# The channel stage of the Fourier branch placed ahead of the recurrence, with its sine block 256 columns wide

## The chip, the cores and the metric

The kernel runs on one core of a Trainium2 chip. The metric is the device time of one execution in microseconds (us); lower is better. The engines are TensorE (PE in the rows, with its weight loads as PEld), VectorE (DVE), ScalarE (ACT), GpSimd (POOL) and SyncE (SP), which here issues the data transfers (DMAs). Each works through its own list of instructions in a fixed order and waits where an operand or a buffer is not ready.

## What is computed

One encoder layer, applied with the same weights to two sequences: the prompt (512 positions) and the sample (1024 positions), 1024 features each. Cut to the part that matters here:

```python
h = rms_norm(x, g_pre_mix) * (1 + sc1) + sh1          # modulation from silu(c) @ w_ada
xa, ya, xb, ga, gb = split(h @ w_in)
xa    = depthwise_conv(xa, conv_w, conv_b, left=2)     # width 4
h_fwd = rg_lru(xa, ..., reverse=False)                 # a first-order recurrence over positions,
h_bwd = rg_lru(xa, ..., reverse=True)                  # gates from two 128x128 products per head
y_a   = ((h_fwd + h_bwd) * gelu(ya)) @ w_a_out
y_b   = fourier_mix(xb) @ w_b_out                      # real 2-D DFT over (positions, 128 channels of a group)
x     = x + gt1 * rms_norm((sigmoid(ga)*y_a + sigmoid(gb)*y_b) @ w_o, g_post_mix)
# then a second sub-layer: h @ w_up, width-3 conv, gelu(gate)*value, @ w_down, norm, gate, residual
```

## The kernel before

All products are made with fp32 data in three passes. An operand is split into a rounded high part and the rest (`split`): the high part is written by ScalarE (L109) or VectorE (L111, a cast), the low part always by VectorE (L112, a subtraction). A pass is high x high, high x low or low x high.

The program is a list of steps. A step is one weight tile ("unit", 128 x 1024 fp32, 512 KB), its matmuls (`mm`) and what is done with the result (`post`). `emit` writes the steps out one after the other into all engines' lists at once. When it comes to a step it first prepares (splits) the units up to three steps ahead, and raw tiles are loaded some further ahead. So the place of a step in the list fixes the order of its work on every engine, and an instruction that waits holds up all that follow it on its engine. Tiles in memory come from a pool of 40 shared buffers (`big`), tiles of TensorE results from a pool of four (`ps`). All DMAs of weights and activations go through SP's list.

The mixer of each sequence is built by `mix` as one list of steps, in this order:

- `mix_heads`: per group of features (4 groups for the prompt, 8 for the sample) a projection to the recurrence input (`w_xa`, then the convolution, L649 on ScalarE and L657 on VectorE), one for each of the gates of the merge (`w_ga`, `w_gb`; L736 on ScalarE, then written out to memory), and a recurrence step (`lru_step`). That has its matmuls, tanh, exp and square root on ScalarE and, put off by up to one step, products and two scans on VectorE (L702, L705, L714 to L722).
- `pq_steps`, the channel stage of the Fourier branch: four steps. For each feature block the positions of the projected rows are paired, x[t] + x[n-t] and x[t] - x[n-t] (`pair_up`: VectorE L800, L803, L804, the high part by ScalarE L109, the low part by VectorE L112). The paired blocks `eh`, `el` are the stationary operand against a table `wxb` (made at the start from the input weights, `wxf`, and written to memory). Each of 8 feature blocks takes, per 128 output positions, three matmuls on the cosine columns (260) and three on the sine columns (252), and three matmuls of one row of output. The rows `hr` are loaded by `ld` (L832). Its results, `pq`, wait for `dft_steps`.
- `ya_steps`: the gelu gate of the recurrence output (`w_ya`), ready for the merge.
- `dft_steps`: the transform over positions, from `pq`.

After that come `merge_steps` (the outputs of both branches, L986 to L997) and the output projection. Within `pq_steps`, the pairing of step j is attached to the step that stands two before it (`PAIR_AHEAD`), and its load to the step three before it.

For the sample, 34 steps of another kind (`ada_steps`, which multiply the conditioning for the later gates on VectorE, L337) are put between the mixer's steps by a list of positions (`place`).

Of the kernel before, what the change touches and what calls it, by code (L numbers as in the profile page):

```python
# [11 lines left out]
F32R = mybir.dt.float32r  # L12
AF = mybir.ActivationFunctionType
# [7 lines left out]
DFF = 2816  # L21
FT = DFF // 128
GRP = 4
NPQ = 512
NCOS = 260
HALF = 258
WIDE = 1032
# [45 lines left out]
class Enc:  # L73
# [175 lines left out]
    def setup(self):  # L249
        nc, a = self.nc, self.a  # L250
        self.hrow = {q.name: self.dram([KT, 128, q.n], "hrow" + q.name) for q in (self.p, self.s)}
        self.wxb = self.dram([KT, 128, NPQ], "wxb")
        self.ident = self.const.tile([128, 128], F32, name="ident")
# [135 lines left out]
    def fold_in(self, tiles, out, ks):  # L389
        nc = self.nc  # L390
        for k in ks:
            ps = self.ps([128, 2, 512])
            v = ps[:, 0, :].rearrange("p (g c) -> p g c", g=4)
            for g in range(4):
                self.mmul(
                    v[:, g, :], lhsT=tiles[g][:, k * 128:(k + 1) * 128], rhs=self.fold,
                    start=True, stop=True)
            w = self.big([128, NPQ], name="wxf")
            nc.scalar.activation(
                out=w[:, 0:252].rearrange("p (g c) -> p g c", g=4), in_=v[:, :, 0:63], func=AF.Copy)  # L400
            nc.scalar.activation(
                out=w[:, 260:512].rearrange("p (g c) -> p g c", g=4), in_=v[:, :, 65:128], func=AF.Copy)
            nc.vector.tensor_copy(w[:, 252:260].rearrange("p (a g) -> p g a", a=2), v[:, :, 63:65])
            out.append(w)

# [334 lines left out]
    def mix_heads(self, sq, hb, hs, sig, lead=0):  # L740
        xh, xl = (lambda: hb["hi"]), (lambda: hb["lo"])
        xc = {}

        def tiles(g):
            return range(g * sq.nf, (g + 1) * sq.nf)

        def proj(nm, g, post):
            return self.fm_steps(sq, self.a[nm], tiles(g), xh, xl, post, on_act=sq.nf == 1)

        fill = [(nm, g, self.spill_post(sig[w, g])) for g in range(sq.groups) for w, nm in enumerate(("w_ga", "w_gb"))]  # L750
        jobs = []
        for g in range(sq.groups):
            jobs.append(("w_xa", g, lambda ps, g=g: self.conv_a(sq, ps, g, xc)))
            jobs.append(fill.pop(0))
            if g:
                jobs += [g - 1, fill.pop(0)]
        jobs += fill[:1] + [sq.groups - 1] + fill[1:]
        steps = []
        for j in jobs[lead:]:
            if isinstance(j, int):  # L760
                steps.append(self.lru_step(sq, j, xc, hs))
            else:
                steps += proj(*j)
        return jobs[:lead], steps
# [53 lines left out]
    def pq_steps(self, sq, pq, before):  # L818
        nc = self.nc
        steps = []  # L820
        n, nt = sq.n, sq.pq_tiles
        box, eo = {}, []
        parts = (slice(0, NCOS), slice(NCOS, NPQ))
        rows = {}

        def ld(j):
            def f():
                rows[j] = []
                for i in range(2 // sq.nf):
                    k = 2 * j + i  # L830
                    x = self.big([128, sq.nf, n + 2], name="hr")
                    nc.sync.dma_start(  # L832
                        out=x[:, :, 0:n], in_=self.hrow[sq.name][k:k + sq.nf].rearrange("k p n -> p k n"))
                    rows[j].append(x)
            return f

        def pair(j):
            return lambda: self.pair_up(sq, rows.pop(j), eo)
        for j in range(KT // 2):
            u = Unit(self.wxb[2 * j:2 * j + 2].rearrange("k p c -> p k c"), 2 * NPQ, on_act=True)  # L840

            def mm(u=u, j=j):
                if j == 0:
                    box["ps"] = [self.ps([128, 2, 512]) for _ in range(nt // 2 + 1)]
                    box["out"] = [box["ps"][t // 2][:, t % 2, :] for t in range(nt)]
                    box["row"] = box["ps"][-1][0:1, 0, 0:NCOS]
                for i in range(2):
                    k = 2 * j + i
                    hi, lo = eo.pop(0)
                    wh, wl = u.hi[:, i * NPQ:(i + 1) * NPQ], u.lo[:, i * NPQ:(i + 1) * NPQ]  # L850
                    end = k == KT - 1
                    for t in range(nt):
                        for c, cols in enumerate(parts):
                            x = slice(t * 128, (t + 1) * 128)
                            for q, (l, r) in enumerate(((hi, wh), (hi, wl), (lo, wh))):
                                self.mmul(
                                    box["out"][t][:, cols], lhsT=l[:, c, x], rhs=r[:, cols],
                                    start=(k == 0 and c == 0 and q == 0), stop=(end and c == 1 and q == 2),
                                    skip_group_check=True)
                    for q, (l, r) in enumerate(((hi, wh), (hi, wl), (lo, wh))):  # L860
                        self.mmul(box["row"], lhsT=l[:, 1, 0:1], rhs=r[:, 0:NCOS],
                                  start=(k == 0 and q == 0), stop=(end and q == 2))

            def post():
                for t in range(nt):
                    pq[t] = self.big([128, 2, NPQ], F32R, name="pq")
                self.split_all([(pq[t], box["out"][t]) for t in range(nt)])
                r = self.big([1, NCOS], name="row")
                nc.scalar.activation(out=r, in_=box["row"], func=AF.Copy, scale=0.5 / math.sqrt(n))
                pq["row"] = self.big([1, 2, NCOS], F32R, name="rowhl")  # L870
                self.split(pq["row"][:, 0, :], pq["row"][:, 1, :], r)
                box.clear()
            steps.append(Step(mm=mm, unit=u, post=post if j == KT // 2 - 1 else None))
        for j in range(KT // 2):
            st = (before + steps)[len(before) - PAIR_AHEAD + j]
            st.post = self.both(st.post, pair(j))
            st = (before + steps)[len(before) - PAIR_AHEAD - 1 + j]
            st.post = self.both(st.post, ld(j))
        return steps
# [508 lines left out]
def place(main, side, at):  # L1388
    out = []
    side = list(side)  # L1390
    at = sorted(at)
    for i, s in enumerate(main):
        while at and at[0] <= i and side:
            at.pop(0)
            out.append(side.pop(0))
        out.append(s)
    return out + side
# [3 lines left out]
def encoder(ctx: ExitStack, tc: tile.TileContext, a, outs):  # L1401
    nc = tc.nc
    e = Enc(ctx, tc, a, outs)
    p, s = e.p, e.s
# [3 lines left out]
    with tc.manual_schedule():  # L1408
# [5 lines left out]
        pq = {q: {} for q in "ps"}  # L1414
# [3 lines left out]
        fo = {q: {} for q in "ps"}  # L1418

        def mix(q, heads):  # L1420
            out = heads
            out += e.pq_steps(q, pq[q.name], heads)
            out += e.ya_steps(q, h1[q.name], hs[q.name], yb[q.name])
            out += e.dft_steps(q, pq[q.name], z[q.name])
            return out

        first, heads = e.mix_heads(p, h1["p"], hs["p"], sig["p"], lead=3)
        side = [e.cond_step()] + e.ada_steps(2) + [Step(), Step()] + e.gate_steps(p, 0, gate["p", 0])
        steps = mix(p, heads)
        ya = len(steps) - 10  # L1430
        sa, sbt = e.h_steps(s, a["x_sample"], 0, h1["s"])
        steps += weave(e.merge_steps(p, yb["p"], z["p"], sig["p"], mg["p"]), sa, 1, 1)
        steps = place(steps, side, [ya - 10] + [ya + i // 2 for i in range(16)] + [ya + 10] + [ya + 22] * 9)
        steps += weave(e.rows_steps(p, a["w_o"], mg["p"], gate["p", 0], a["x_prompt"], x2["p"]), sbt, 0, 1)

        _, heads = e.mix_heads(s, h1["s"], hs["s"], sig["s"])
        steps += place(mix(s, heads), e.ada_steps(3) + e.ada_steps(4), [*range(28), *range(36, 46)])
        pa, pbt = e.h_steps(p, x2["p"], 1, h2["p"])
        steps += weave(e.merge_steps(s, yb["s"], z["s"], sig["s"], mg["s"]),
                       e.gate_steps(s, 0, gate["s", 0]) + pa, 8, 1)  # L1440
# [126 lines left out]
```

## Time and profile before

| | us |
|---|---|
| median of 3 runs | 2152.92 (2151.53 to 2154.18) |
| the profiled execution, its own time | 2154.59 |
| its span, first to last instruction | 2152.8 |
| TensorE busy | 2086.5 (97%) |
| VectorE busy | 1433.5 (67%) |
| ScalarE busy | 928.4 (43%) |
| GpSimd busy | 54.5 (3%) |

The profiled execution is one run, so durations taken from it are to be set against its own 2154.59 us, of which 1.8 us lie outside the span. "Busy" counts an engine as busy while an instruction of its own is under way; matmuls overlap and their ends are modelled, so the distance between the starts of successive matmuls is the better measure of their cost. A mark such as `[8.51 <-ACT th L683]` behind a row says that the engine stood idle 8.51 us before it and what released it. PEclk is the clock granted to TensorE as a share of full speed.

### The profile page before, as it was taken

Reading aid. Unit: us, or ns where it says so; the run is one execution under the profiler, and the core shown is the slowest. Engines: PE = TensorE matmul, PEld = TensorE weight load, DVE = VectorE, ACT = ScalarE, POOL = GpSimd, SP = SyncE. Lnnn points to the kernel's source line nnn. Section 1 sums busy time; section 2 is a strip of 40 time slices with the busy share of each in tenths; the row PEclk is TensorE's granted clock in tenths of the full one; section 3 lists DMA queues with packets and bytes.
Section 4 is the critical chain, followed back from the end, with each engine's and each line's share of the span. In section 5 each row is a group of like instructions: output and inputs, shape, how many; then the busy total and the mean of one; then the engine's idle time right before and its main releaser. Section 6 shows DMA issues by size and latency. Waiting matters only on the chain.

```text
span 2152.8 us, 24316 instructions
## 1 busy us (share of the span) xinstructions
PE 2086.5 (97%) x9602; PEld 1704.4 (79%) x9602; DVE 1433.5 (67%) x1816; ACT 928.4 (43%) x1195; POOL 54.5 (3%) x124
## 2 busy tenths in 40 slices
PE   7997799999999789999999999999999999999998
PEld 6886688888888668888888888888888888888887
DVE  4785788666776654656757546557788888875543
ACT  2447345345646532224533334643334444454442
POOL 0000010100000000000000000100000000000000
PEclk9998799999999889999999999999999999999999
DMA  9444366533232321453544323432122222285422
GB/s 340 155 147 146 113 227 217 202 108 112 85 99 92 130 86 59 148 175 111 184 155 137 108 98 125 140 127 88 50 88 79 79 81 86 72 300 176 162 93 107
DMA packets 91121, 284.52 MB, mean 132 GB/s; under 512 B 9056, under 2 KB 20736, under 8 KB 91008
## 3 DMA queue, kind: packets, MB, share of 16 engines
q1 hardware_dynamic: 91008, 282.98, 38.2%
q8 instruction: 75, 1.23, 0.2%
q14 instruction: 38, 0.31, 0.0%
HBM read 237.84 MB, written 45.11 MB: 131 GB/s over the span
## 4 chain that ended last, share of the span: by engine, by line
PE 90%; DVE 4%; ACT 3%; issue 1%; DMA 1%; POOL 0%; SPq 0%; DVEq 0%; POOLq 0%; ACTq 0%
PE ps L201 89%; PE ps L204 1%; ACT th L683 1%; DVE hl L112 0%; DVE th L714 0%; DVE th L719 0%; ACT th L693 0%; DVE el L112 0%; ACT eh L109 0%; ACT ea L691 0%; DMA hr<-hrowp 0%; DVE th L717 0%; DMA wxbt<-in_wxbT_dram 0%; DVE eo L804 0%; ACT xn L412 0%
## 5 line engine op out<-in xcount | busy, mean ns | idle before, releaser
L201 PE MATMUL ps<-hh,hl 128*128 128x512 f32 x2144 | 631.8, 394 | 0.0
L201 PEld LDWEIGHTS ps<-hh,hl 128*128 128x128 f32 x2144 | 402.4, 188 | 94.7 <-DVE hl L112 0.2
L201 PE MATMUL ps<-hl,ah 128*128 128x512 f32 x1440 | 453.1, 396 | 0.0
L112 DVE TENSOR_TENSOR hl<-raw,hl 128x1024 fp32r<-128x1024 f32 (+2 forms) x240 | 287.3, 1200 | 163.9 <-ACT hl L109 161.4
L201 PE MATMUL ps<-hl,hl 128*128 128x512 f32 x1072 | 380.7, 394 | 0.0
L201 PE MATMUL ps<-hx,wq 128*128 128x512 f32 x1596 | 370.7, 394 | 0.0
L201 PEld LDWEIGHTS ps<-hx,wq 128*128 128x128 f32 x1596 | 299.6, 188 | 71.0 <-DVE wq L1248 0.2
L109 ACT ACTIVATE hl<-raw 128x1024 fp32r<-128x1024 f32 x204 | 213.6, 1053 | 265.6 <-PE ps L201 238.5
L201 PEld LDWEIGHTS ps<-hl,ah 128*128 128x128 f32 x1440 | 268.9, 188 | 62.2
L201 PE MATMUL ps<-hl,al 128*128 128x512 f32 x720 | 283.9, 394 | 0.0
L201 PEld LDWEIGHTS ps<-hl,hl 128*128 128x128 f32 x1072 | 201.3, 188 | 47.2
L201 PEld LDWEIGHTS ps<-hl,al 128*128 128x128 f32 x720 | 135.2, 188 | 32.3
L1344 DVE SCALAR_TENSOR_TENSOR cf<-ps,vec,cf 128x511 f32<-128x511 f32 (+1 forms) x100 | 75.3, 808 | 83.6 <-ACT cf L1336 83.3
L201 PE MATMUL ps<-yh,hl 128*128 128x512 f32 x384 | 112.3, 395 | 0.6 <-DVE hl L112 0.5
L201 PE MATMUL ps<-hl,eh 128*128 128x260 f32 (+2 forms) x224 | 58.7, 363 | 43.3 <-ACT eh L109 30.4
L1192 DVE SCALAR_TENSOR_TENSOR cf<-cq,vec,cf 128x1023 f32<-128x1023 f32 x76 | 97.1, 1277 | 0.0
L1247 ACT ACTIVATE wq<-wsum 128x512 fp32r<-128x512 f32 x76 | 46.1, 629 | 118.0 <-DVE wsum L1258 118.0
L201 PEld LDWEIGHTS ps<-yh,hl 128*128 128x128 f32 x384 | 71.5, 188 | 17.8 <-DVE hl L112 1.0
L1336 ACT ACTIVATE cf<-ps,vec 128x512 f32<-128x512 f32 (+1 forms) x50 | 39.1, 826 | 105.6 <-PE ps L201 105.6
L201 PEld LDWEIGHTS ps<-hl,eh 128*128 128x128 f32 (+1 forms) x224 | 46.5, 250 | 47.7 <-ACT eh L109 32.5
L112 DVE TENSOR_TENSOR al<-fq,ah 128x512 fp32r<-128x512 f32 x88 | 57.2, 686 | 35.2 <-PE ps L201 18.5
L736 ACT ACTIVATE sg<-ps 128x1024 f32<-128x1024 f32 x24 | 24.7, 1028 | 114.1 <-PE ps L201 114.0
(181 smaller groups left out, 2432.8 us busy)
## 6 DMA issues: line engine op xcount, KB each, us to landing
raw<-in_w_up_dram SPq DMA_DIRECT2D x88, 512.0 KB, 3.5
raw<-in_w_down_dram SPq DMA_DIRECT2D x66, 512.0 KB, 3.5
ada<-in_w_adaT_dram SPq DMA_DIRECT2D x32, 512.0 KB, 4.7
raw<-in_w_o_dram SPq DMA_DIRECT2D x24, 512.0 KB, 3.5
fs<-cf SPq DMA_DIRECT2D x22, 512.0 KB, 2.6
fq<-fs SPq DMA_DIRECT2D x22, 512.0 KB, 6.4
ada<-in_w_ada_dram SPq DMA_DIRECT2D x16, 512.0 KB, 8.7
raw<-in_w_gb_dram SPq DMA_DIRECT2D x16, 512.0 KB, 4.3
```

The lines of the kernel that those rows point to most:

```text
L109: nc.scalar.activation(out=hi, in_=src, func=AF.Copy)
L112: nc.vector.tensor_tensor(out=lo, in0=src[:, 0:keep], in1=hi[:, 0:keep].bitcast(F32), op=ALU.subtract)
L201: self.nc.tensor.matmul(*args, **kw)
L204: self.nc.tensor.transpose(*args)
L683: nc.scalar.activation(out=t[:, f, :], in_=ps[:, f, :], func=AF.Tanh, scale=0.5, bias=self.halfb[:, b:b + 1])
L736: self.nc.scalar.activation(out=t, in_=ps, func=AF.Tanh, scale=0.5)
L1192: nc.vector.scalar_tensor_tensor(out=box[key][:, o], in0=c[:, i], scalar=self.vec[:, V_FW + 3 * m + t:V_FW + 3 * m + t + 1], in1=box[key][ ...
L1247: nc.scalar.activation(out=hi, in_=src, func=AF.Copy)
L1336: nc.scalar.activation(out=acc[:, f, :], in_=ps[:, f, :], func=AF.Identity, scale=w[:, 1:2], bias=self.vec[:, V_FB + m:V_FB + m + 1])
L1344: nc.vector.scalar_tensor_tensor(out=acc[:, f, o], in0=ps[:, f, o.start + d:o.stop + d], scalar=w[:, tap:tap + 1], in1=acc[:, f, o], op0=A ...
```

## The change

Four things. The channel stage is no longer put behind all heads but behind the first four head steps of the prompt and the first three of the sample, so that its pairing and loads are attached to those. The sine columns of the table are moved from 260:512 to 264:516, with four zero columns (written by GpSimd) ahead of them; the sine matmul reads 256 columns and writes result columns 256:512, where the zeros are added to the last four cosine columns. In the prompt's job list two entries are exchanged (the first recurrence step and the projection that followed it), so that the first four prompt steps hold no recurrence. And the positions of the conditioning steps in the sample's list are shifted.

```diff
-NPQ = 512
+NPQ = 516
...
-                out=w[:, 260:512].rearrange("p (g c) -> p g c", g=4), in_=v[:, :, 65:128], func=AF.Copy)
+                out=w[:, 264:516].rearrange("p (g c) -> p g c", g=4), in_=v[:, :, 65:128], func=AF.Copy)
+            nc.gpsimd.memset(w[:, 260:264], 0.0)
...
         jobs += fill[:1] + [sq.groups - 1] + fill[1:]
+        if lead:
+            jobs[4], jobs[5] = jobs[5], jobs[4]
...
-        parts = (slice(0, NCOS), slice(NCOS, NPQ))
+        parts = ((slice(0, NCOS), slice(0, NCOS)), (slice(NCOS, NPQ), slice(256, 512)))
...
-                        for c, cols in enumerate(parts):
+                        for c, (wcols, cols) in enumerate(parts):
...
-                                    box["out"][t][:, cols], lhsT=l[:, c, x], rhs=r[:, cols],
+                                    box["out"][t][:, cols], lhsT=l[:, c, x], rhs=r[:, wcols],
...
-            out = heads
-            out += e.pq_steps(q, pq[q.name], heads)
+            at = 4 if q is p else 3
+            out = heads[:at] + e.pq_steps(q, pq[q.name], heads[:at]) + heads[at:]
...
-        steps += place(mix(s, heads), e.ada_steps(3) + e.ada_steps(4), [*range(28), *range(36, 46)])
+        steps += place(mix(s, heads), e.ada_steps(3) + e.ada_steps(4), [0, 1, 2, *range(7, 34), *range(36, 46)])
```

The counts of instructions are the same on TensorE, VectorE, ScalarE and SP; GpSimd has eight more. What moves, on TensorE, in the prompt: before, the channel stage (operands `eh`, `el`) follows the matmuls of the last recurrence step (`xch`, `xcl`).

```order
L201 MATMUL ps_1674<-xcl_1361,hl_1532 128x512
L201 MATMUL ps_1674<-xch_1360,hl_1532 128x512
L201 MATMUL ps_1716<-hl_1563,eh_1631 128x260 x2
L201 MATMUL ps_1716<-hl_1563,el_1632 128x260
L201 MATMUL ps_1716<-hl_1563,eh_1631 128x252 x2
```

Now it follows the projection for the second merge gate (`hh`, `hl` are the parts of the normalised input).

```order
L201 MATMUL ps_904<-hh_735,hl_835 128x512 x2
L201 MATMUL ps_904<-hl_736,hl_835 128x512
L201 MATMUL ps_904<-hh_735,hl_835 128x512
L201 MATMUL ps_986<-hl_865,eh_933 128x260 x2
L201 MATMUL ps_986<-hl_865,el_934 128x260
L201 MATMUL ps_986<-hl_865,eh_933 128x256 x2
```

The two pieces show the same stage start some 360 rows earlier in TensorE's list, behind a gate projection.

On VectorE, in the prompt: before, the pairing (L800 to L804 and the low part `el`) stands between pieces of the last recurrence step (L702 to L722).

```order
L804 TENSOR_TENSOR eo_1697<-hr_1635 128x2x256
L112 TENSOR_TENSOR el_1701<-eo_1697,eh_1700 128x1024
L702 SCALAR_TENSOR_TENSOR th_1655<-th_1655,xc_1351 128x1024
L702 SCALAR_TENSOR_TENSOR th_1675<-th_1675,xc_1351 128x1024
L705 SCALAR_TENSOR_TENSOR th_1655<-ea_1684,th_1655 128x1024
L705 SCALAR_TENSOR_TENSOR th_1675<-ea_1690,th_1675 128x1024
L112 TENSOR_TENSOR hl_1711<-raw_1566,hl_1711 128x1024
L800 COPY hr_1704<-hr_1704 128x2
L803 TENSOR_TENSOR eo_1749<-hr_1704 128x2x256
L804 TENSOR_TENSOR eo_1749<-hr_1704 128x2x256
L112 TENSOR_TENSOR el_1753<-eo_1749,eh_1752 128x1024
L714 TENSOR_TENSOR th_1655<-th_1655,th_1645 128x1024
```

Now only splits of units (`hl`) stand between two pairings.

```order
L112 TENSOR_TENSOR hl_865<-raw_801,hl_865 128x1032
L112 TENSOR_TENSOR hl_899<-raw_820,hl_899 128x1032
L803 COPY hr_896<-hr_896 128x2
L806 TENSOR_TENSOR eo_930<-hr_896 128x2x256
L807 TENSOR_TENSOR eo_930<-hr_896 128x2x256
L112 TENSOR_TENSOR el_934<-eo_930,eh_933 128x1024
L112 TENSOR_TENSOR hl_940<-raw_838,hl_940 128x1032
L803 COPY hr_937<-hr_937 128x2
```

And the last recurrence step of the prompt now stands among the units of `ya_steps` and the conditioning steps (L337); lines from L400 on have moved by one to three.

```order
L112 TENSOR_TENSOR hl_1830<-raw_1738,hl_1830 128x1024
L703 SCALAR_TENSOR_TENSOR th_1846<-th_1846,xc_1558 128x1024
L703 SCALAR_TENSOR_TENSOR th_1866<-th_1866,xc_1558 128x1024
L706 SCALAR_TENSOR_TENSOR th_1846<-ea_1875,th_1846 128x1024
L706 SCALAR_TENSOR_TENSOR th_1866<-ea_1881,th_1866 128x1024
L112 TENSOR_TENSOR hl_1892<-raw_1769,hl_1892 128x1024
L337 SCALAR_TENSOR_TENSOR adap_1897,mod<-ada_1694,cs_1497 128x1024
L715 TENSOR_TENSOR th_1846<-th_1846,th_1836 128x1024
L718 SCALAR_TENSOR_TENSOR th_1836<-ea_1875,th_1846 128x512 x2
L715 TENSOR_TENSOR th_1866<-th_1866,th_1856 128x1024
L720 SCALAR_TENSOR_TENSOR th_1856<-ea_1881,th_1866 128x512 x2
```

What was beside the pairing before is thus beside the gelu gate's units now.

On SP, in the prompt, the loads of the paired rows (`hr`) now stand behind four table tiles, each of which waits for a raw buffer.

```order
L124 DMA raw_838<-wxb 128x2x516
L124 DMA raw_868<-wxb 128x2x516
L835 DMA hr_896<-hrowp 128x2x512
L738 DMA sgp_68<-sg_803 128x1024
L124 DMA raw_902<-in_w_lru_p_dram 128x1024
```

Before, the first load of `hr` also stood behind the fourth table tile; there it was issued beside the last recurrence step, now beside the gate projections.

## Rows read from the trace of the kernel before

**Rows 1.** The page's chain that ended last: shares of the span by engine

```profile
PE 90%; DVE 4%; ACT 3%; issue 1%; DMA 1%; POOL 0%; SPq 0%; DVEq 0%; POOLq 0%; ACTq 0%
```

**Rows 2.** Stretches: length, PE, PEld, DVE, ACT, POOL busy (counts), clock, DMA share, GB/s

```profile
195.36:247.82 52.46, 27.04 (x122) 23.36 (x121) 28.96 (x32) 25.11 (x31) 0.00 (x0) 0.64 0.42 143
719.24:776.13 56.89, 35.66 (x217) 32.87 (x217) 36.90 (x44) 27.45 (x28) 0.00 (x0) 0.73 0.36 118
247.82:308.06 60.24, 60.24 (x279) 49.47 (x277) 50.09 (x82) 24.33 (x31) 2.21 (x4) 1.00 0.51 173
...
776.13:900.00 123.87, 123.87 (x622) 104.17 (x621) 59.01 (x85) 32.13 (x42) 0.00 (x0) 1.00 0.28 95
```

**Rows 3.** TensorE's timeline, sample's channel stage: start, duration, engine, line, tiles, idle before

```profile
749.55 0.63 PE L201 MATMUL ps<-hl,eh 128*128 128x252 f32 x2
...
750.19 0.64 PE L201 MATMUL ps<-hl,eh 128*128 128x260 f32 x2
...
753.77 0.41 PE L201 MATMUL ps<-hl,eh 128*128 128x260 f32 x2
...
754.13 0.40 PE L201 MATMUL ps<-hl,eh 128*128 128x252 f32 x2
...
754.49 0.28 PE L201 MATMUL ps<-hl,eh 128*128 128x260 f32 x1
```

**Rows 4.** TensorE's timeline, a start in each channel stage that waited long

```profile
204.05 0.80 PE L201 MATMUL ps<-hl,eh 128*128 128x260 f32 x2 [8.51 <-ACT th L683]
...
766.05 0.80 PE L201 MATMUL ps<-hl,eh 128*128 128x260 f32 x2 [8.93 <-ACT eh L109]
```

**Rows 5.** VectorE's timeline, one pairing of the prompt

```profile
199.31 0.17 DVE L800 COPY hr<-hr 128x2 f32<-128x2 f32 x1 [6.92 <-DMA hr<-hrowp]
...
203.07 1.22 DVE L112 TENSOR_TENSOR hl<-raw,hl 128x1024 fp32r<-128x1024 f32 x1
204.21 0.16 DVE L800 COPY hr<-hr 128x2 f32<-128x2 f32 x1
```

**Rows 6.** Timelines of ScalarE and VectorE in the first prompt heads

```profile
83.67 1.03 ACT L736 ACTIVATE sg<-ps 128x1024 f32<-128x1024 f32 x1 [9.64 <-PE ps L201]
...
85.91 0.69 DVE L111 CAST hl<-raw 128x1024 fp32r<-128x1024 f32 x1
```

**Rows 7.** Timeline of ScalarE in the first sample heads

```profile
429.93 1.03 ACT L736 ACTIVATE sg<-ps 128x1024 f32<-128x1024 f32 x1 [9.93 <-PE ps L201]
...
441.07 1.21 ACT L649 ACTIVATE xc<-ps,vec 128x1024 f32<-128x1024 f32 x1 [9.17 <-PE ps L201]
```

**Rows 8.** SP's timeline, first load of hr; summary line of all 12 loads

```profile
191.69 0.46 SPq L832 DMA_DIRECT2D hr<-hrowp  x1
...
DMA to landing us min/median/max: 3.2/4.7/9.9
```

**Rows 9.** VectorE's timeline, one recurrence step of the prompt

```profile
89.63 2.36 DVE L702 SCALAR_TENSOR_TENSOR th<-th,xc 128x1024 f32<-128x1024 f32 x2
...
97.03 1.22 DVE L705 SCALAR_TENSOR_TENSOR th<-ea,th 128x1024 f32<-128x1024 f32 x1 [2.98 <-ACT ea L691]
...
101.35 1.23 DVE L714 TENSOR_TENSOR th<-th,th 128x1024 f32<-128x1024 f32 x1 [1.23 <-ACT th L709]
...
109.62 0.69 DVE L111 CAST hl<-raw 128x1024 fp32r<-128x1024 f32 x1
```

**Rows 10.** VectorE's timeline, the merge's first product of the prompt

```profile
308.26 1.22 DVE L997 SCALAR_TENSOR_TENSOR mg<-sg,ps 128x1024 f32<-128x1024 f32 x1
```

**Rows 11.** VectorE's timeline, the convolution in the first sample heads

```profile
442.31 3.92 DVE L657 SCALAR_TENSOR_TENSOR xc<-ps,vec,xc 128x1022 f32<-128x1022 f32 x3 [8.01 <-ACT xc L649]
...
448.14 1.22 DVE L112 TENSOR_TENSOR hl<-raw,hl 128x1024 fp32r<-128x1024 f32 x1
```

**Rows 12.** Groups of GpSimd by form: one of its four memsets

```profile
L1556 POOL MEMSET const-bfloat16-1.0<- 128x1 bf16 x1 | 0.1, 102 | 0.0
```

**Rows 13.** Waits of SP's queue: total, times, longest

```profile
SPq L832 <- PE ps L201: 8.1, 1, 8.1
```

More of the change, by code (lines that the diff above doesn't have):

```diff
@@ L865, in post @@
                 for t in range(nt):
-                    pq[t] = self.big([128, 2, NPQ], F32R, name="pq")
+                    pq[t] = self.big([128, 2, 512], F32R, name="pq")
                 self.split_all([(pq[t], box["out"][t]) for t in range(nt)])
```

## The prediction

> **What bounds the kernel now.** I read the chain that ended last first: TensorE holds 90% of it [rows 1], so the time is what TensorE needs plus what it waits. The list of TensorE's waits by length leads to two places with waits above 8 us, 204.05 in the prompt and 766.05 in the sample [rows 4], both in the channel stage. The reader is to see that one waits for ScalarE's tanh of a recurrence step (its result buffers are taken) and the other for a high part of a pairing. The stretches of the two channel stages then give their size [rows 2]: in the prompt 52.46 us with TensorE busy for 27.04 at a mean clock of 0.64, in the sample 56.89 us with 35.66 at 0.73. Right behind each, TensorE is busy without a gap at clock 1.00.
>
> How much of this is needed? At full clock six matmuls start within 754.49-753.77 = 0.72 us, three on 260 columns (0.36 to 754.13) and three on 252 (0.36): 0.12 us each [rows 3]. While the clock is at its lower level (1.2 of 2.4 GHz), after waits, three take 750.19-749.55 = 0.64, or 0.215 each. The prompt has 8 blocks x (2 tiles x 2 halves x 3 + 3) = 120 matmuls, 14.4 us; the sample 8 x (4 x 2 x 3 + 3) = 216, 25.9 us. So 38.1 and 31.0 us are lost, 69.1 together: the most that any placing of this stage can give.
>
> The loss has a plain cause. One pairing runs 3.76 us from its copy to the end of its low part (199.31 to 203.07, with ScalarE's high part in the middle), and with one unit's low part behind it the next begins at 204.21, 4.9 us later [rows 5]. The prompt needs four, the sample eight. 4 x 4.9 is 20 us and not 52: the rest is recurrence work in between on VectorE's and ScalarE's lists.
>
> **The change part by part.** All from the profiled execution, 2154.59 us, 1.67 above the median of the runs.
>
> *Prompt, the stage itself.* Now it follows two gate projections. The first ends at about 83.65 (ScalarE's eviction starts at 83.67 [rows 6]); a group of 48 matmuls on 512 columns takes 441.07-429.93 = 11.1 us in the sample [rows 7] and has the same count here, so TensorE is free at 94.8. VectorE ends the split before at 85.91 [rows 6] and writes two low parts of 1.14 by 88.2. The first hr load stands on SP's queue behind the fourth table tile, which waits for the first of those low parts, so it is issued near 87.5. The like load took 199.31-191.69 = 7.6 us until VectorE could go on [rows 5, 8], so the first pairing starts at 95.1 and the second, one pairing and one low part later, at 100.0. The third load stands behind a tile whose buffer is freed at 100.0; between the median landing of 4.7 [rows 8] and 7.6 I take 6.2, so it starts at 106.2, and the fourth at 111.1. The last low part is there at 114.9, and 28 matmuls (3.4 us) follow: 118.3, which makes 23.5 us after 94.8 against 52.46: 29.0 saved. With landings of 3.2 throughout the stage takes 17.8 us, with 9.9 it takes 29.5 [rows 8]: 34.7 to 23.0 saved.
>
> *Prompt, what becomes late.* First, the recurrence steps come closer: two groups and the step's own matmuls (22.2 + 5.55 us) lie between the first and the second. In such a step VectorE stands 2.98 and 1.23 us for ScalarE [rows 9], which reaches TensorE where nothing else is left to do: 0 to 4.2, I take 2.4. Second, the last recurrence step's VectorE work, 4.7 us (four of about 1.2) and 109.62-101.35 = 8.27 [rows 9], 13.0 in all, was beside the pairings and now lies beside the gelu gate's units. There VectorE is already busy for 50.09 of 60.24 us [rows 2], so 10.15 are free: between 2.9 us (all free time is used) and 13.0 (none is) come back to TensorE as late splits, since TensorE has no gap of its own there. Units are split three steps ahead, which lets it use some of it; I take the middle, 8.0. Third, the merge's products wait at 308.26 for VectorE [rows 10]; if it is still late then, up to the 4.7 of the first half of a recurrence step, taken as 2.4. So 12.8 come back (2.9 to 21.9), and the prompt gains 16.2.
>
> *Sample.* The projection before the stage ends at 441.07 [rows 7], and VectorE idles 8.01 us before the convolution that follows it at 442.31 [rows 11]. The first step's pairings can be made in that time (the loads are issued a step earlier), so its 54 matmuls run at once, to 447.5. VectorE is in the convolution and its split until 448.14 [rows 11]; then six pairings of 3.76 and two low parts of 1.14 end at 473.0, and 25 matmuls at 476.0. That is 34.9 us against 56.89: 22.0 saved, less about 1 for matmuls at the lower clock after waits. If it all ran at that clock (216 x 0.215 = 46.4) 10.5 would be saved; if nothing waited, 31.0. What is moved behind it, the last recurrence step beside the gelu gate, has cover: VectorE is busy for only 59.01 of 123.87 us there [rows 2]. I take 21.0.
>
> *The wider sine block.* 4 more columns on 48 matmuls of the prompt and 96 of the sample. 252 and 260 columns take the same 0.36 us per three [rows 3], so I take 0; in proportion to columns it would be 144 x 0.12 x 4/256 = 0.27 us, and a gain of the like size is possible below. The table's tiles grow by 0.8%, in transfers that are not waited for. Eight small memsets of about 0.10 us [rows 12] stand on GpSimd in the lead-in, nothing waits for GpSimd there but the norms: 0, at most 0.8.
>
> The Trainium skill (SBUF — State Buffer, section "Who interferes with whom") says that GpSimd and VectorE share one pair of ports under an exclusive lock. The memsets could thus hold VectorE's copies in the lead-in for as long as they last, 0.8 us; with that the sum would be 36.4 and not 37.2. No row of before has such a memset beside a VectorE copy.
>
> *Sum.* 16.2 + 21.0 + 0 = 37.2. 2154.59 - 37.2 = 2117.4 for a profiled execution, and 1.67 less for the median: **2115.7 us**.
>
> **The rivals.**
>
> *VectorE gives little back.* If the three-step lead covers all but the 2.9 and neither other wait comes, the prompt gains 26.1 and the sample 22.0: 2104.8. For it: TensorE had no gap at all in 247.82 to 308.06 although VectorE was 83% busy. Against: the work comes in one block of 8.27 us.
>
> *VectorE gives much back.* All 21.9 of the prompt's bounds (7.1 left), and the sample midway to the lower clock (16.3): 2129.5. For it: in-order lists pass every block on. Against: all three must happen.
>
> *Everything is hidden.* The pairings vanish beside the gate projections and both stages run at their bare 14.4 and 25.9: 69.1 less, 2083.8. For it: VectorE's 8.01 idle before 442.31. Against: the stage is too short for its pairings, 20 and 30 us of VectorE. The Trainium skill (Perfetto Trace Analysis, section "Optimization Strategy") says that regimes with different busiest engines gain by interleaving; by that rule alone one would expect this case, and rows 2 show such regimes, but the stage is still in one piece.
>
> *Slower: the shared buffers run short.* The pq tiles are now held through the recurrence steps, four tiles and two rows in the sample, and every recurrence step takes eight or more buffers of the same 40. If a load waits for one in each of the 12 recurrence steps that now follow, it decides from 37.2/12 = 3.1 us per step. The one buffer wait of this kind on SP was 8.1 us [rows 13]; at that, 97.2 - 37.2 = 60.0 us slower, 2212.9. Against: the rows of hr and pairs go earlier, and those are most of what the stage holds.
>
> *The change doesn't do what it says.* The wait only moves: loads behind raw tiles make the early stage as long as the late one was. Then 2152.9. Against: even landings of 9.9 leave 29.5 us.
>
> **How the numbers follow.** Forecast 0.50 (own range 2106 to 2126); little given back 0.20; much given back 0.18; everything hidden 0.03; buffers short 0.05; no effect 0.04. The ends of the bounds are (34.7 - 2.9) + 31.0 = 62.8 and (23.0 - 21.9) + 10.5 = 11.6, that is 2090.1 and 2141.3; the range for 8 in 10 is a little inside, 2096 to 2139. Faster by over 0.2% (about 4.3 us, what a measurement of this kernel can tell from no change): the first four, 0.91; within it 0.04; slower 0.05.
>
> **What would show it.** TensorE's channel stage of the prompt near 95 to 118 us and of the sample near 441 to 476, with waits for el, eh and hr there and none for a recurrence's tanh. The pairing's starts 4.9 to 6.2 us apart in the prompt. Then waits of TensorE for low parts of units (hl) in the prompt's gelu stage of 8 us in all, where there are none now; 10 us or more in the whole prompt speaks for my give-back, under 4 for the first rival, over 18 for the second. No gap in the sample's gelu stage. The forecast is wrong if TensorE's waits behind the moved stages exceed the 50 us saved in them, or if SP shows buffer waits of over 3 us in the recurrence steps.

## The result and the profile after

The changed kernel takes 2118.6 us (median) against about 2153 before: a ratio of 0.984 with an interval of 0.9818 to 0.9863. The forecast was 2115.7. One execution of each kernel, of 2634.8 and 2308.9 us, was in a slower state and is left out. By the medians the gain is 34.3 us; the profiled executions stand 2154.59 - 2118.58 = 36.0 us apart, since the one before lies 1.67 above its median. The forecast's sum was 37.2. The kernels of the experiments are compared with 2118.6 and with runs of the kernel before beside them (2152.9 to 2153.0).

The two stretches of the channel stage, with the gelu stage of the prompt between them, in the profile after (columns as in [rows 2]):

```profile
93.41:117.44 24.03, 17.84 (x121) 15.68 (x121) 18.14 (x24) 7.15 (x8) 0.00 (x0) 0.86 0.63 210
...
225.00:289.78 64.78, 57.81 (x255) 45.95 (x254) 54.12 (x74) 30.42 (x38) 1.37 (x2) 0.97 0.43 152
...
425.98:461.32 35.34, 28.73 (x215) 26.28 (x214) 26.16 (x35) 11.50 (x13) 0.00 (x0) 0.95 0.36 130
```

The prompt's stage fell from 52.46 to 24.03 us and the sample's from 56.89 to 35.7 (425.62 to 461.32 by the starts of its first matmul and of the next step's). ScalarE is busy for only 7.15 us in the first, where it was busy for 25.11: the recurrence is gone from it. But the gelu stage, without a gap at clock 1.00 before, now has 7 us of gaps at a clock of 0.97 (it starts at 220.15, 4.9 us ahead of the stretch shown).

VectorE's pairings in the prompt, one row for the start of each (timeline; compare the 199.31 row of [rows 5]):

```profile
94.02 0.17 DVE L803 COPY hr<-hr 128x2 f32<-128x2 f32 x1 [6.86 <-DMA hr<-hrowp]
...
99.04 0.17 DVE L803 COPY hr<-hr 128x2 f32<-128x2 f32 x1
...
104.02 0.16 DVE L803 COPY hr<-hr 128x2 f32<-128x2 f32 x1
...
110.04 0.17 DVE L803 COPY hr<-hr 128x2 f32<-128x2 f32 x1 [0.31 <-DMA hr<-hrowp]
```

The reader is to see a chain with nothing else in it but one unit's split per pairing, and ahead of it 6.86 us in which VectorE waits for a load. The third load was not late; the fourth hardly.

TensorE's first wait in the prompt's stage, and some of its longer waits behind the stage (timeline):

```profile
96.71 0.80 PE L201 MATMUL ps<-hl,eh 128*128 128x260 f32 x2 [3.14 <-ACT eh L109]
...
149.62 0.47 PE L201 MATMUL ps<-xch,hl 128*128 128x512 f32 x1 [1.45 <-DVE xc L658]
...
246.02 0.80 PE L201 MATMUL ps<-hh,hl 128*128 128x512 f32 x1 [2.90 <-DVE hl L112]
...
277.65 0.73 PE L201 MATMUL ps<-yh,hl 128*128 128x512 f32 x2 [1.50 <-DVE hl L112]
...
295.85 0.39 PE L201 MATMUL ps<-z,hl 128*128 128x258 f32 x1 [0.70 <-DVE mg L1000]
...
300.82 0.50 PE L201 MATMUL ps<-yh,hl 128*128 128x512 f32 x1 [1.20 <-DVE yb L991]
```

From 149 on all of these name VectorE: the price of the move, none over 3 us. All of TensorE's waits from 117.44 up to the sample's mixer make 11.65 us; two of them, 0.28 and 0.64, name ScalarE.

What stands on VectorE ahead of the longest of them, at 246.02, is the second half of the last recurrence step and behind it a conditioning product (L337), and only then the low part that TensorE waits for:

```profile
235.33 1.23 DVE L715 TENSOR_TENSOR th<-th,th 128x1024 f32<-128x1024 f32 x1
...
243.60 1.22 DVE L337 SCALAR_TENSOR_TENSOR ada<-ada,cs 128x1024 f32<-128x1024 f32 x1
...
244.74 1.22 DVE L112 TENSOR_TENSOR hl<-raw,hl 128x1024 fp32r<-128x1024 f32 x1
```

From 235.33 to 243.60 that half takes the 8.27 us of [rows 9]. In the sample the convolution still stands on VectorE between the first step's pairings and the rest:

```profile
427.06 3.92 DVE L658 SCALAR_TENSOR_TENSOR xc<-ps,vec,xc 128x1022 f32<-128x1022 f32 x3 [1.95 <-ACT xc L650]
...
432.88 0.15 DVE L803 COPY hr<-hr 128x1 f32<-128x1 f32 x1
```

To see where the 36 us come from, the same events are looked up in both traces: ScalarE's first eviction of the prompt's recurrence input, its first of the sample's, and the sample's last gelu. Before:

```profile
66.96 1.45 ACT L649 ACTIVATE xc<-ps,vec 128x512 f32<-128x512 f32 x2 [4.07 <-PE ps L201]
...
418.79 1.21 ACT L649 ACTIVATE xc<-ps,vec 128x1024 f32<-128x1024 f32 x1 [8.42 <-PE ps L201]
...
865.33 1.03 ACT L773 ACTIVATE gl<-ps 128x1024 f32<-128x1024 f32 x1 [7.69 <-PE ps L201]
```

and after:

```profile
65.84 1.45 ACT L650 ACTIVATE xc<-ps,vec 128x512 f32<-128x512 f32 x2 [4.12 <-issue]
...
403.49 1.21 ACT L650 ACTIVATE xc<-ps,vec 128x1024 f32<-128x1024 f32 x1 [8.74 <-PE ps L201]
...
830.08 1.02 ACT L776 ACTIVATE gl<-ps 128x1024 f32<-128x1024 f32 x1 [7.74 <-PE ps L201]
```

The distance of the first two, the prompt's mixer and projection, fell from 351.8 to 337.7 (14.2), that of the last two from 446.5 to 426.6 (20.0). 1.1 us stem from the lead-in, whose work is not touched but for eight memsets and a table 4 columns wider, and 1.0 from all that stands behind the last event. That makes the 36.2 us between the two spans, 2152.8 and 2116.6.

### The profile page after: what moved, and what is told of

Same layout as the page of the kernel before. It is cut to its first block, busy times and chain, and to the rows that moved or that the text cites. A ratio compares the mean times of both kernels' runs of the same rounds, so it can differ in the third digit from the quotient of the medians.

```text
span 2116.6 us, 24327 instructions
## 1 busy us (share of the span) xinstructions
PE 2073.9 (98%) x9602; PEld 1691.0 (80%) x9602; DVE 1433.9 (68%) x1816; ACT 929.2 (44%) x1195; POOL 53.7 (3%) x132
## 3 DMA queue, kind: packets, MB, share of 16 engines
q8 instruction: 75, 1.23, 0.2%
## 4 chain that ended last, share of the span: by engine, by line
PE 78%; issue 0%; DVE 0%; ACT 0%; DVEq 0%; POOLq 0%; POOL 0%; ACTq 0%
PE ps L201 77%; PE ps L204 1%; ACT eh L109 0%; DVE el L112 0%; DVE eo L806 0%; DVE eo L807 0%; DVE ro L1099 0%; DVEq L1565 0%; POOLq L1565 0%; ACT junk L1080 0%; POOL sm L1082 0%; ACTq L1565 0%; DVE hr L803 0%; DVEq L806 0%; ACTq L109 0%
## 5 line engine op out<-in xcount | busy, mean ns | idle before, releaser
L109 ACT ACTIVATE hl<-raw 128x1024 fp32r<-128x1024 f32 (+1 forms) x204 | 213.9, 1053 | 267.8 <-PE ps L201 236.5
L201 PE MATMUL ps<-hx,hl 128*128 128x512 f32 x288 | 67.0, 394 | 0.0
L201 PE MATMUL ps<-yl,hl 128*128 128x512 f32 x192 | 65.4, 394 | 0.8 <-DVE yl L112 0.8
```

The source lines that it names most:

```text
L109: nc.scalar.activation(out=hi, in_=src, func=AF.Copy)
L201: self.nc.tensor.matmul(*args, **kw)
```

## The experiments

The theory: a channel stage lasts as long as VectorE and ScalarE need for its pairings and for what stands between them in their lists; away from the recurrence that is less, and part of it comes back where VectorE is short of time.

**The parts of the change.** The wide sine block at the old place (`NPQ`, the memset, `parts` and the pq tiles as in the change, nothing else):

> The wider sine block alone, at the old place. Theory (the gain is the channel stage taken away from the recurrence's work): no difference, 2153.5 within 2 us of the kernel before. Rival (the 256 columns or the shifted table speed the matmuls up): 144 sine matmuls would have to gain 35 us, about 0.24 us each, so a time near 2120.

2152.84 us, ratio to the kernel before 0.9998 (0.9988 to 1.0008). The width, its memsets and the larger table cost and bring nothing that can be measured, which here means no more than about 2 us.

The move with the sine block left at 252 columns:

> The move with the exchange of two entries and the shifted conditioning steps, but the sine block 252 columns wide as before. Theory: as the changed kernel, 2118.6 within 2 us. Rival (the width matters): clearly above 2120.

2118.41 us, ratio 0.9838 (0.9823 to 0.9852): the whole gain is the move.

One sequence at a time:

```diff
-            at = 4 if q is p else 3
+            at = 4 if q is p else len(heads)       # prompt alone; conditioning positions as before
```

> Changed kernel with the sample's channel stage and conditioning positions back at the old place. Theory: the prompt's part alone, by the sample's first convolution in the two traces 418.79 - 403.49 = 15.3 us less than before, so 2138. Rival (the gain is in the sample, the prompt gives all back in the gelu stage): 2150 or more.

2140.97 us, ratio 0.9943 (0.9929 to 0.9958): 12.0 us, some 3 less than expected, but far from the rival's 2150. Between the events above the prompt has its 14.0 us here too (337.87); the sample, left as it was, takes 1.0 us longer than before (447.58).

```diff
-            at = 4 if q is p else 3
+            at = len(heads) if q is p else 3       # sample alone; jobs[4], jobs[5] not exchanged
```

> Changed kernel with the prompt's channel stage and job order back as before. Theory: 35 - 15.3 = about 20 us less than before, so 2133. Rival (both parts share one gain, for example through the clock): not additive with the prompt's part, 2125 or 2145.

2130.9 us, ratio 0.9897 (0.9882 to 0.9912). The two parts bring 12.0 and 22.0 us, together 34.0, and both at once 34.3: they add up, so the rival of one shared gain fell, and the sample's is the larger.

**What makes a stage long.** The exchange of two entries undone, so that a recurrence step stands ahead of the prompt's stage:

```diff
-        if lead:
-            jobs[4], jobs[5] = jobs[5], jobs[4]
...
-            at = 4 if q is p else 3
+            at = 5 if q is p else 3
```

> Changed kernel without the exchange of two entries: in the prompt the first recurrence step stands ahead of the channel stage (gate, recurrence, gate, channel stage). Theory (VectorE's recurrence work between the pairings makes the stage long): its 13 us of VectorE work stand before the first pairing, which would start near 109 instead of 94 while TensorE is ready at 99, so the prompt's stage takes 31 to 33 us instead of 24 and the time is 2125 to 2128. Rival (any place ahead of the other recurrences is as good): 2118.6 within 2 us.

2126.88 us, ratio 0.9878 (0.9863 to 0.9892), 8.3 us above the changed kernel. The size is as expected, the picture a little different: the first pairing was to start near 109, and it starts at 101.29. VectorE's timeline in that kernel:

```profile
103.91 1.22 DVE L112 TENSOR_TENSOR el<-eo,eh 128x1024 fp32r<-128x1024 f32 x1 [1.12 <-ACT eh L109]
106.27 1.23 DVE L715 TENSOR_TENSOR th<-th,th 128x1024 f32<-128x1024 f32 x1 [1.15 <-ACT th L710]
107.53 2.34 DVE L718 TENSOR_TENSOR_SCAN th<-ea,th 128x512 f32<-128x512 f32 x2
...
113.40 1.22 DVE L723 TENSOR_TENSOR th<-th,th 128x1024 f32<-128x1024 f32 x1
...
115.68 0.16 DVE L801 COPY hr<-hr 128x2 f32<-128x2 f32 x1
```

The recurrence's second half stands behind the first pairing and not ahead of it, and TensorE waits for the second:

```profile
118.31 0.80 PE L201 MATMUL ps<-hl,eh 128*128 128x260 f32 x2 [6.91 <-ACT eh L109]
```

This is the wait of [rows 4] in small: recurrence work between two pairings. The stage lasts from 100.5 (103.92 less its wait of 3.41) to 133.99, 33.5 us, against 24.0 without it.

**What comes back, and why.** The 16 conditioning products of the prompt's gelu stage cut to 64 columns:

```diff
+                c = slice(0, 64 if job == 2 else 1024)
                 nc.vector.scalar_tensor_tensor(
-                    out=out, in0=w, scalar=0.5, in1=self.cvec[s], op0=ALU.mult, op1=ALU.mult,
+                    out=out[:, c], in0=w[:, c], scalar=0.5, in1=self.cvec[s][:, c], op0=ALU.mult, op1=ALU.mult,
```

> Changed kernel in which the 16 conditioning products that stand in the prompt's gelu stage run over 64 instead of 1024 columns (so that conditioning vector is wrong): about 16 x 1.15 = 18 us less VectorE work there, nothing else changed. Theory (what comes back in the prompt is VectorE short of time in the gelu stage and behind it): TensorE's waits there of 7.5 us and the merge's 2.7 go, the time falls to 2109. Rival (they come from ScalarE's part of the last recurrence step, or from the units' place): 2118.6 within 2 us.

2110.91 us, ratio 0.9805 (0.979 to 0.9819), 7.7 us below the changed kernel. Of TensorE's waits in the gelu and merge stages one of more than 0.6 us is left, the first:

```profile
245.30 0.50 PE L201 MATMUL ps<-hh,hl 128*128 128x512 f32 x1 [1.87 <-DVE hl L112]
```

What came back in these two stages was, but for this wait at most, VectorE's lack of time: the units' place and ScalarE's part of the last recurrence step, the rivals, are as in the changed kernel. The same without leaving anything out, by placing those products one to a step from eight steps earlier:

```diff
-... [ya - 10] + [ya + i // 2 for i in range(16)] + [ya + 10] + [ya + 22] * 9)
+... [ya - 10] + [ya - 8 + i for i in range(16)] + [ya + 10] + [ya + 22] * 9)
```

> Changed kernel in which the prompt's 16 conditioning products stand one to a step from eight steps before the gelu stage on, instead of two to a step within it: half of them, 8 x 1.22 = 10 us of VectorE work, leave the stage. Theory (VectorE has about 7.5 us too much to do in the gelu stage): TensorE's waits there shrink by 6, the time is 2112 to 2114. Rival (VectorE is as short of time between the recurrence steps, so the wait only moves ahead): 2118.6 within 2 us.

2110.1 us, ratio 0.9799 (0.9785 to 0.9814): 8.5 us less, more than expected. The same waits went (one of 1.74 and one of 1.20 us are left there), and the steps between the recurrences did not get new ones; the rival fell.

**What is left in the stages.** The prompt's row loads ahead of the last two table tiles on SP's queue:

```diff
             st = (before + steps)[len(before) - PAIR_AHEAD - 1 + j]
-            st.post = self.both(st.post, ld(j))
+            if sq.nf == 2:
+                st.loads = [*st.loads, ld(j)]
+            else:
+                st.post = self.both(st.post, ld(j))
```

> Changed kernel with the prompt's four row loads (hr) issued together ahead of the last two table tiles. Theory (VectorE idles 6.9 us at 87 to 94 for the first of these loads, then for the fourth a little): the pairings start near 88 instead of 94, the stage falls from 24 to 18 us, the time to 2113. Rival (what is saved there comes back in the gelu stage, where VectorE is short anyway): 2118.6 within 2 us.

2114.1 us, ratio 0.9817 (0.98 to 0.9833), 4.5 us less. The first pairing no longer waits for its load, and the stage, from 95.36 to 112.86, takes 17.5 us instead of 24.0:

```profile
87.87 1.23 DVE L112 TENSOR_TENSOR hl<-raw,hl 128x1032 fp32r<-128x1032 f32 x1
89.01 0.16 DVE L803 COPY hr<-hr 128x2 f32<-128x2 f32 x1
```

TensorE's waits in the gelu stage stay as they were (2.90 us at the longest in both kernels), so what was saved did not come back in the gelu stage: the rival fell.

The sample's stage one head step later:

```diff
-            at = 4 if q is p else 3
+            at = 4                                 # conditioning positions [0, 1, 2, 3, *range(8, 34), ...]
```

> Changed kernel with the sample's channel stage one head step later (behind the first w_gb projection), conditioning positions moved with it. Theory (the sample's stage is as long as its pairings and the convolution of 5.8 us that VectorE makes ahead of six of them): the convolution now lies beside the projection, the stage falls from 35 to about 29 us, the time to 2113. Rival (the pairings alone set it, or the conditioning steps shift the loss): 2118.6 within 2 us.

2119.56 us, ratio 0.9843 (0.9829 to 0.9858): no gain, a miss. The stage, from 439.04 to 473.13, takes 34.1 us and not the 29 expected. VectorE's timeline there says why:

```profile
429.30 3.92 DVE L658 SCALAR_TENSOR_TENSOR xc<-ps,vec,xc 128x1022 f32<-128x1022 f32 x3 [8.02 <-ACT xc L650]
...
435.12 0.15 DVE L803 COPY hr<-hr 128x1 f32<-128x1 f32 x1
```

It idles 8.02 us ahead of the convolution, and all eight pairings come behind it. The convolution had left the stage, but so had the 8 us in which the first two pairings were made. The expectation had counted the one and overlooked the other. With loads and pairings attached one step earlier, on top of the edit before, both are had:

```diff
-            st = (before + steps)[len(before) - PAIR_AHEAD + j]
+            ahead = PAIR_AHEAD + (sq.nf == 1)
+            st = (before + steps)[len(before) - ahead + j]
             st.post = self.both(st.post, pair(j))
-            st = (before + steps)[len(before) - PAIR_AHEAD - 1 + j]
+            st = (before + steps)[len(before) - ahead - 1 + j]
```

> Sample's channel stage one head step later, as in the run before, but its loads and pairings attached three steps ahead instead of two, so that the first step's two pairings are again made before the convolution, in VectorE's idle 8 us. Theory (the run before put the convolution off the stage but the first pairings behind it): six pairings and two low parts from 435, the last low part near 460, stage 439 to 465, so 26 us instead of 35: 2110. Rival (the stage's TensorE work and its ScalarE high parts cannot go faster than 3.8 us a pairing from its start): 2117 or more.

2112.1 us, ratio 0.981 (0.9795 to 0.9824), 6.5 us less. The stage itself, 438.40 to 464.06, takes 25.7 us, the bare 25.9 that the prediction had worked out for its matmuls. A stretch of about its length:

```profile
438.55:464.50 25.95, 25.95 (x219) 25.04 (x218) 19.91 (x28) 11.72 (x14) 0.00 (x0) 1.00 0.43 141
```

TensorE has no gap and its clock is 1.00. That is 10 us less than 35.7, and 10.1 between the events above; the total shows 6.5. Of the 3.5 us that are missing, the lead-in, which ends at 67.17 instead of 65.84, accounts for 1.3 (see the last section).

**All three together:**

> The early row loads of the prompt, the spread conditioning products and the sample's earlier pairings together. Theory (three separate losses): 4.5 + 6 + 9 = about 19 us less than the changed kernel, 2099. Rival (VectorE's total work in the prompt is the limit, so early rows and spread products share one gain): 2103 to 2105.

2092.48 us, ratio 0.9717 (0.9701 to 0.9734) to the kernel before: 60.4 us less than it and 26.1 less than the changed kernel. That is below the theory's 2099 as well as the rival's 2103. TensorE's longest waits in the list of waits (total, times, longest; wxbt and hh are the lead-in):

```profile
PE ps L201 <- DMA wxbt<-in_wxbT_dram: 8.0, 4, 6.6
PE ps L201 <- DVE hl L112: 2.6, 5, 1.8
PE ps L201 <- DVE hh L111: 1.9, 1, 1.9
PE ps L201 <- ACT th L684: 1.9, 2, 1.4
PE ps L201 <- DVE el L112: 1.5, 2, 0.8
```

The three gains are at least additive (4.5 + 8.5 + 6.5 = 19.5 by the runs); between the events used above, early rows and spread products bring 6.1 and 9.9 in the prompt by themselves and 15.5 together, the sample's part 10.1 by itself and 12.1 together. So early rows and spread products don't share one gain: the rival fell.

## Why the prediction was right, step by step

| step | predicted, us | measured, us |
|---|---|---|
| prompt's stage | 23.5 (saves 29.0) | 24.0 (28.4) |
| starts of its pairings | 95.1, 100.0, 106.2, 111.1 | 94.0, 99.0, 104.0, 110.0 |
| late at the recurrence steps | 2.4 | 2.0 |
| late in and behind the gelu stage | 8.0 | 7.0 |
| late in the merge | 2.4 | 2.7 |
| prompt, net | 16.2 | 14.2 in the traces, 12.0 alone |
| sample's stage | 34.9 (saves 22.0) | 35.7 (21.2) |
| sample, net | 21.0 | 20.0 in the traces, 22.0 alone |
| wide sine block | 0 | 0.1 (within 2) |
| sum | 37.2 | 36.0 between the profiles, 34.3 by the medians |

*The bound.* That the stages were long by what stood between their pairings is shown by the run with a recurrence ahead (24.0 to 33.5 us), and that the pairings themselves then set them by the runs with early rows and earlier pairings.

*The loads.* The step that put the first load near 87.5, with 7.6 us until VectorE could go on, held: it is issued at 86.45 and VectorE goes on 7.57 us later, in a kernel whose lead-in ended 1.1 us earlier. Behind it two errors cancel. The third load was assumed to land late, so that its pairing would start 6.2 us behind the second; it started 5.0 behind. The fourth was put 4.9 us behind the third and came 6.0 behind, since the split between them has its cast on VectorE (0.69 us) and the load was 0.31 us late. That the stage comes so near its 23.5 us is in part luck.

*What comes back.* The three sizes are sums of TensorE's waits in the trace after: from 117.44 to 246, to 284 and to 301 us. The mechanisms are the ones named. In the recurrence step ahead of the wait of 1.45 us VectorE stands 2.98 and 1.23 us for ScalarE as in [rows 9], and the short conditioning products leave that wait as it was (1.44); in the gelu and merge stages they show that VectorE is the cause. But the three middle values were choices between wide bounds (0 to 4.2, 2.9 to 13.0, 0 to 4.7), and that each came out within 1 us is in part luck.

The sum of what comes back was too small. The prompt gives back 28.4 - 14.2 = 14.2 and not 12.8, and the waits, less the 1.15 of before in the same steps, make only 10.5 of it. The trace shows the other 3.7 in the distances between the starts of matmuls. From the end of the wait of 2.90 us on the granted clock is 0.50, the lower level (1.2 of 2.4 GHz), for 3.4 us, and matmuls on 512 columns start 0.43 us apart instead of 0.23 (the stretch, then TensorE's timeline):

```profile
245.73:249.15 3.42, 3.13 (x7) 2.48 (x8) 3.38 (x6) 0.00 (x0) 0.00 (x0) 0.50 0.61 194
```

```profile
247.46 1.05 PE L201 MATMUL ps<-hh,hl 128*128 128x512 f32 x2
248.32 0.63 PE L201 MATMUL ps<-hl,hl 128*128 128x512 f32 x1
...
249.40 0.40 PE L201 MATMUL ps<-hl,hl 128*128 128x512 f32 x1
```

The eight matmuls from 246.02 to 249.40 take 3.38 us where 8 x 0.23 would be 1.84: 1.5 us. The other 2.2 stand for the most part around the waits themselves, some 0.1 to 0.4 us at each, where the starts on both sides are farther apart than the marked wait and the usual distance make. The prediction had a term of 1 us for this in the sample and none in the prompt.

*The sample.* Its stage holds as worked out: the first step's pairings ahead of the convolution, the other six from 432.88 on, their last low part done at 458.1. Behind the stage no wait of TensorE is marked up to the last gelu, as forecast.

*The rivals.* Little and much given back (2104.8 and 2129.5) are both off: TensorE's waits after the prompt's stage are 11.65 us (1.15 of them there before), between the 10 and the 18 named for the forecast and the second rival. "Everything is hidden" is not what this change does, but its time was in reach: with pairings made beside other projections the sample's stage is at its bare length. Its sum went by the stages alone, and the kernel with all three edits is 8.7 us above its 2083.8. By the Trainium skill (Perfetto Trace Analysis, section "Optimization Strategy"), interleaving regimes with different busiest engines may gain; the run with the sample's pairings a step earlier agrees, 35.7 to 25.7 us for the stage. The wait for shared buffers did not come. The longest of this kind in SP's list of waits after is a load for the merge, outside the recurrence steps, of 5.2 us; the kernel before had the like (L945, 5.1):

```profile
SPq L948 <- PE ps L201: 5.2, 1, 5.2
```

The 8.1 us of [rows 13] are gone. The prediction called it the one wait of its kind, but the list before has two more for the same loads, 6.7 us released by `el` and 5.3 by `eo`; they are gone too. How near the 40 buffers are to their limit no run shows. The lock between GpSimd and VectorE that the Trainium skill names (SBUF — State Buffer, section "Who interferes with whom") would cost 0.8 us at most here; the wide block alone came out 0.1 us below the kernel before, within an interval of about 2 us, so no run here can show it.

## What to carry to other kernels

Where engines work through lists in fixed order, a stage that starves TensorE is often not short of an engine's time but has other work between its links: count the bare links (here 4 x 4.9 and 8 x 3.8 us) and compare with the stage. Links made ahead of the stage bound it no longer (17.5 us in the run with early rows, 25.7 in the one with earlier pairings). When such a stage is moved, price both ends: what it now stands beside, and what the work it left now stands beside; a window whose helper engine is 83% busy has room for a part of it only, and side work that has no due time is what to move out of there. Waits cost more than their marked length (here 14.2 us came back, 10.5 of them marked as waits). A step moved behind a barrier-like instruction (a convolution that waits for a projection) may lose idle time that it used before.

## What was not expected of the hardware

The lead-in ends up to 1.9 us later or earlier in kernels whose lead-in has the same work: the first eviction of the recurrence input starts at 65.84 in the changed kernel, at 66.96 before, and in the one with early rows at

```profile
67.78 1.45 ACT L650 ACTIVATE xc<-ps,vec 128x512 f32<-128x512 f32 x2 [4.12 <-issue]
```

Part of it may be TensorE's longest wait for a table's DMA, 6.1 us in the changed kernel's list of waits and 6.6 in the kernels with early rows and with all three edits; but the kernel before has 5.8 there and is later than the changed one, so the cause stays open. Each figure is of one execution. Differences of 1 to 2 us between such kernels are therefore compared by events behind the lead-in, as above.
